# The first half-FFN of a two-layer backbone: latents and context as one operand of 768 tokens, by block products

## The chip, the cores and the metric

The kernel runs on one core of a Trainium2 chip. The metric is the device time of one execution in microseconds (us). TensorE (PE in the profile) multiplies matrices, VectorE (DVE) and ScalarE (ACT) work on SBUF and PSUM, GpSimd (POOL) does little here, and SyncE (SP) issues all loads and stores, in order. Results of TensorE land in 8 PSUM banks of 128 x 512 fp32 values.

## The reference

512 latent tokens `x` and 256 context tokens `ctx`, of width 1024, pass two layers. Each layer is a half-step SwiGLU, a token mixer (layer 0: a bidirectional HGRN2 over context and latents; layer 1: a chunked spatial-gating MLP), and a second half-step SwiGLU. The part that is changed is the first half-FFN of layer 0, for both streams with the same weights:

```
def modulate(x, m, k):                       # m = silu(cond) @ w_mod + b_mod, 9 chapters of 1024
    return x * (1 + m[3*k+1]) + m[3*k]
def swiglu(h, w_in, w_out):
    gate, up = split(h @ w_in, 2)            # w_in 1024 x 5632, w_out 2816 x 1024
    return (silu(gate) * up) @ w_out
x   = layer_norm(alpha * x   + mx[2] * 0.5 * swiglu(modulate(x,   mx, 0), w_in, w_out))
ctx = layer_norm(alpha * ctx + mc[2] * 0.5 * swiglu(modulate(ctx, mc, 0), w_in, w_out))
```

`mx` comes from the conditioning `c`, `mc` from `c_ctx`; both use the same `w_mod`. Behind it the HGRN2 reads the modulated latents and context.

## The kernel before

fp32 products are made of three matmuls each (`mm3`): an operand is split into a rounded part (ScalarE copies it, L135) and the rest (VectorE subtracts, L136), and hi x hi, hi x lo and lo x hi are added in PSUM. `unit` loads one weight tile of 128 x 1024 (512 KB) into a ring of 3 (`raw`) and splits it into a ring of 6 (`w`).

The hidden width is 22 blocks of 128; a block f needs two units (gate 2f, up 2f+1), each of 8 k-slices. `FeedIn` makes the products of a block plainly: 2 x 8 x 3 matmuls of 128 x 512 for the latents (`psf<-xm,w`), then `evac`: silu of the gate bank on ScalarE, times the up bank on VectorE, kept in SBUF as `h`. `FeedContext` does the same with 256 columns (`psf<-xmc,w`). The order before is: latent feed, latent `OutPhase`, context feed, context `OutPhase`, HGRN values (`psv`). So both weights are loaded and split twice. `OutPhase` runs 22 steps (2 halves of the output columns x 11 pairs of blocks); a step loads one unit of `w_out`, splits two blocks (`hs`), and makes 6 matmuls of 128 x 512 per token tile (`y<-w,hs`). At its end each token tile is gated, added, normalised (`evac`, `norm`) and transposed (`pt`) into the next operand.

At the start the operand is made k by k: two modulation rows per k (chapters 1 and 0) are multiplied with silu(c) on VectorE (`mod_dot`, two half dots of 512 and a read of the accumulator), and the columns scale and shift the transposed tokens. The first six units are staged: their products are made k by k in six banks as the slices of `xm` arrive. The other modulation chapters are queued and taken a row at a time (`mod_step`) between blocks.

The later half-FFNs use `FeedSums`: two units that share a block are combined so that seven products of blocks (half of k by 256 columns) replace eight (`seven`). It needs sums of operand blocks (`f4` to `f7`, made once in `sum_steps`) and of weight halves per pair (`weight_sums`, four half-width operations on VectorE), and keeps four partial banks in `sc`. Per pair of units 84 matmuls replace 96. In the second half-FFN of layer 0 (`f2`) the operand's blocks `bw` have eight tiles of their own.

A scheduler orders the instructions of each engine within the program order and the pools; a tile's slot is reused when all its readers are done. The names: `xm`/`xmc` the split operands, `hs` the split products, `mraw`/`mw` modulation rows, `raw`/`rawu` gate and up weights as loaded, `e` a weight sum, `psf` plain banks, `psc`, `pse`, `psa`, `psb` banks of `seven`.

Of the kernel before, what the change touches and what calls it, by code (L numbers as in the profile page):

```python
# [1 line left out]

# [36 lines left out]
SEG = NT + NTC  # L39
NLATE = 4  # L40
# [30 lines left out]
def backbone_kernel(  # L71
# [92 lines left out]
    def mod_dot(pool, dst, w, s):  # L164

        n = D // 2
        for i in range(2):
            c = slice(i * n, (i + 1) * n)
            junk = pool.tile([P, n], BF16, tag="junk", name="junk", bufs=2)
            nc.vector.scalar_tensor_tensor(junk, w[:, c], 1.0, s[:, c], ALU.mult, ALU.mult, dst[:, i : i + 1])  # L170

    def mod_task(modp, srow, l, ch, conds):
        accs = {c: modp.tile([P, KD, 2], F32, tag=f"acc_{c}", name=f"acc_{c}", bufs=2) for c in conds}
        for f in range(KD):
            raw = modp.tile([P, D], F32, tag="mraw", name="mraw", bufs=2)
            nc.sync.dma_start(raw, mod_w[l, ch, f])
            for c in conds:
                mod_dot(modp, accs[c][:, f, :], raw, srow[c])
            yield
        for c in conds:  # L180
            key = (l, ch, c)
            dot = modp.tile([P, KD], F32, tag="dot", name="dot", bufs=2)
            nc.vector.reduce_sum(dot, accs[c], axis=AX.X)
# [14 lines left out]
    class Scraps:  # L198
# [5 lines left out]
        def tile(self, shape, dtype, tag, name, bufs=1):  # L204
            if tag == "mraw":
                return self.pool.tile(shape, dtype, tag=self.ring, name=self.ring, bufs=2)
            got = self.got.setdefault(tag, [0])
            n = int(np.prod(shape[1:])) * (2 if dtype == BF16 else 4) // 4
# [393 lines left out]
    class Forms:  # L602
# [7 lines left out]

        def place_forms(self, new_block):
            self.new_block, self.blocks, self.place = new_block, {}, ExitStack()
# [40 lines left out]
        def blocks_of(self, xm):  # L653
            h = KD // 2
            return (xm[:, :, k0 : k0 + h, c0 : c0 + 2 * P] for k0, c0 in ((0, 0), (h, 0), (h, 2 * P)))
# [9 lines left out]
        def seven(self, xm, sp, raw0, raw1, sc, early=None):  # L665
# [5 lines left out]
            K2, N2 = D // 2, 2 * P  # L671
# [16 lines left out]
            def raws():  # L688
# [4 lines left out]
                return g, u, sp.tile([P, D], F32, tag="e", name="e", bufs=2)  # L693
# [114 lines left out]
    class HgrnValues(Phase):  # L808
# [7 lines left out]
        def load(self):  # L816
            self.ws = [unit(hg_wi[0, kk]) for kk in range(4)]
# [155 lines left out]
    xm = new_xm(xmp, "xm", T)  # L973
    L0 = ExitStack()
    xcp = L0.enter_context(sbuf(name="xcp", bufs=1))
    xmc = new_xm(xcp, "xmc", TC)

    with sbuf(name="hp", bufs=1) as hp, sbuf(name="modp", bufs=1) as modp:
        nc.scalar.preload_act_table(AF.Silu)
        srow = {"x": silu_row(modp, "x")}  # L980

        f0 = FeedIn(0, 0, xm, NT, 6)
        with sbuf(name="first", bufs=1) as fp:
            cols = fp.tile([P, KD, 2], F32, name="cols")
            f0.open()
# [5 lines left out]

            def feed(k):
                acc = fp.tile([P, 2, 2], F32, tag="acc", name="acc", bufs=2)
                xt = fp.tile([P, T], F32, tag="xt", name="xt", bufs=3)
                for ch in (1, 0):
                    m = fp.tile([P, D], F32, tag="mw", name="mw", bufs=6)
                    for c in ((slice(0, D // 2), slice(D // 2, D)) if k == 0 else (slice(0, D),)):
                        nc.sync.dma_start(m[:, c], mod_w[0, ch, k][:, c])
                    mod_dot(modp, acc[:, ch, :], m, srow["x"])
# [8 lines left out]
            bias = fp.tile([P, KD, 2], F32, name="bias")  # L1008
            for ch in range(2):
                nc.vector.tensor_scalar(bias[:, :, ch], mbT[:, 0, ch, :], float(ch), None, ALU.add)  # L1010
            for k in range(KD):
                acc, xt = fed if k == 0 else feed(k)
                nc.vector.reduce_sum(cols[:, k, :], acc, axis=AX.X)
                nc.vector.tensor_tensor(cols[:, k, :], cols[:, k, :], bias[:, k, :], ALU.add)
# [3 lines left out]
                else:  # L1018
# [4 lines left out]
                    xf = fp.tile([P, T], F32, name="xf")  # L1023
                    nc.vector.tensor_scalar(xf, xt, cols[:, k, 1:2], cols[:, k, 0:1], ALU.mult, ALU.add)
                    latest[0] = nc.vector.tensor_tensor(xm[:, 1, k, :], xf, hi.bitcast(F32), ALU.subtract)
# [9 lines left out]
            products(KD - 1, staged)  # L1035
        nc.sync.dma_start(lnT, ln_T)
        srow["c"] = silu_row(modp, "c")
        for ch in (2, 4, 3):
            queue_mod(modp, srow, 0, ch, ["x", "c"])
        for ch in (1, 0):  # L1040
            queue_mod(modp, srow, 0, ch, ["c"])
        for l, ch in ((0, 5), (0, 7), (0, 6), (0, 8), (1, 2)):
            queue_mod(modp, srow, l, ch, ["x"])
        hget = f0.rest(hp, 2)
        with bpools() as bp:

            def context_operand():
                sc, sh = made((0, 1, "c")), made((0, 0, "c"))
                for k in range(KD):
                    ct = bp.tile([P, TC], F32, tag="ct", name="ct", bufs=2)  # L1050
                    nc.sync.dma_start(ct, ctxT[k])
                    nc.vector.tensor_scalar(ct, ct, sc[:, k : k + 1], sh[:, k : k + 1], ALU.mult, ALU.add)
                    split(xmc[:, 0, k, :], xmc[:, 1, k, :], ct)

            f1 = FeedContext(0, 0, xmc, NTC)
            xm = new_xm(xmp, "xm", T)
            OutPhase(
                hget, NF, ffn_units(0, 0), NT, 0, 0, "x", 0.5, lambda t: x[t], False, (0, 1),
                xm, lambda t: x1[t], f1,
            ).run(bp, context_operand, 1)  # L1060
            hget = f1.rest(hp, 0.5)
            for ch in (5, 7, 6):
# [564 lines left out]
```

## Time and profile before

| | |
|---|---|
| three runs | 2439.37, 2439.59, 2440.41 us; median 2439.59 |
| profiled execution | span 2438.5 us (the page gives its span; no other time of it is recorded) |
| TensorE, weight loads | 2410.2 us (99%), 2187.7 us (90%) |
| VectorE, ScalarE, GpSimd | 1959.6 us (80%), 1174.1 us (48%), 35.7 us (1%) |
| chain that ended last | TensorE 91%, VectorE 5% |
| transfers | 366 MB, 150 GB/s over the span |

A line of a group reads: line of the kernel, engine, operation, tile written <- tiles read, shapes, count | busy us, mean ns of one | idle time before them and what ended it. A timeline row reads: start, duration, engine, line, operation, in brackets the idle time before. Row of stretches: for each engine the busy time and the number of instructions, then granted clock, share of the DMA engines and GB/s.

### The profile page before, as it was taken

How to read it: one execution, taken by the hardware profiler on the slowest of the kernel's cores; microseconds unless marked ns; L12 is line 12 of the kernel's file. 1: busy time of each engine (PE TensorE's matmuls, PEld its weight loads, DVE VectorE, ACT ScalarE, POOL GpSimd, SP SyncE). 2: the span in 40 equal slices, each digit the busy share in tenths (PEclk: the TensorE clock that was granted, in tenths of full speed). 3: DMA queues.
4: the chain of work that ended last, by engine and by line, in shares of the span. 5: the costliest groups of instructions: out<-in, count | busy, mean ns of one | idle time of the engine just before them, and what ended most of it. 6: DMA issues, size and time to landing. Idle time of an engine off the chain costs nothing.

```text
span 2438.5 us, 38322 instructions
## 1 busy us (share of the span) xinstructions
PE 2410.2 (99%) x14979; PEld 2187.7 (90%) x14979; DVE 1959.6 (80%) x3522; ACT 1174.1 (48%) x1830; POOL 35.7 (1%) x57
## 2 busy tenths in 40 slices
PE   7999999999999999999999999999999999999998
PEld 5888889988889888999988999988999988999987
DVE  7965678786488886988896988898888887988785
ACT  4222434454355452555643555534666643555641
POOL 0000000000000000000000000000000000000000
PEclk9999999999999999999999999999999999999999
DMA  8866555874212213433474333574322365333452
GB/s 322 293 211 204 167 177 184 290 259 158 70 53 62 65 48 113 160 107 108 145 234 151 104 105 104 163 247 155 116 87 92 124 234 163 132 112 104 139 165 77
DMA packets 107431, 366.04 MB, mean 150 GB/s; under 512 B 12472, under 2 KB 13808, under 8 KB 107248
## 3 DMA queue, kind: packets, MB, share of 16 engines
q1 hardware_dynamic: 107248, 363.58, 45.2%
q8 instruction: 117, 1.92, 0.3%
q14 instruction: 66, 0.54, 0.1%
HBM read 350.92 MB, written 12.61 MB: 149 GB/s over the span
## 4 chain that ended last, share of the span: by engine, by line
PE 91%; DVE 5%; DMA 1%; ACT 1%; issue 1%; POOL 0%; SPq 0%; DVEq 0%; POOLq 0%; ACTq 0%
PE y L150 9%; PE y L148 9%; PE y L149 9%; PE psf L150 5%; PE psf L148 5%; PE psf L149 5%; PE psc L148 5%; PE psc L150 5%; PE psc L149 5%; PE pse L150 3%; PE pse L148 3%; PE pse L149 2%; PE psa L149 1%; PE psa L150 1%; PE psa L148 1%; PE psq L150 1%
## 5 line engine op out<-in xcount | busy, mean ns | idle before, releaser
L135 ACT ACTIVATE w<-raw 128x1024 fp32r<-128x1024 f32 (+3 forms) x447 | 435.1, 976 | 399.0 <-DMA raw<-in_ffn_w_in 85.3
L136 DVE TENSOR_TENSOR w<-raw,w 128x1024 fp32r<-128x1024 f32 (+3 forms) x447 | 499.5, 1121 | 154.6 <-ACT w L135 153.6
L148 PE MATMUL y<-w,hs 128*128 128x512 f32 x984 | 383.7, 390 | 0.0
L150 PE MATMUL y<-w,hs 128*128 128x512 f32 x984 | 383.1, 389 | 0.2 <-DVE hs L136 0.2
L149 PE MATMUL y<-w,hs 128*128 128x512 f32 x984 | 382.9, 389 | 0.0
L135 ACT ACTIVATE hs<-h 128x512 fp32r<-128x512 f32 (+1 forms) x220 | 125.9, 587 | 198.6 <-PE y L150 181.0
L150 PEld LDWEIGHTS y<-w,hs 128*128 128x128 f32 x984 | 184.6, 188 | 39.6 <-DVE hs L136 1.2
L149 PEld LDWEIGHTS y<-w,hs 128*128 128x128 f32 x984 | 184.7, 188 | 38.2
L148 PEld LDWEIGHTS y<-w,hs 128*128 128x128 f32 x984 | 184.7, 188 | 38.2
L148 PE MATMUL psf<-xm,w 128*128 128x512 f32 (+1 forms) x544 | 191.3, 356 | 14.6 <-ACT xm L1021 11.0
L150 PE MATMUL psf<-xm,w 128*128 128x512 f32 (+1 forms) x544 | 192.4, 354 | 1.3 <-DVE w L136 1.2
L149 PE MATMUL psf<-xm,w 128*128 128x512 f32 (+1 forms) x544 | 192.1, 354 | 0.4 <-DVE xm L136 0.4
L136 DVE TENSOR_TENSOR hs<-h,hs 128x512 fp32r<-128x512 f32 (+1 forms) x220 | 134.9, 632 | 68.7 <-ACT hs L135 68.6
L148 PE MATMUL psc<-f,w 128*128 128x256 f32 x560 | 159.0, 284 | 0.9 <-ACT sc L728 0.9
L150 PE MATMUL pse<-f,w 128*128 128x256 f32 x560 | 158.8, 283 | 0.0
L148 PE MATMUL pse<-f,w 128*128 128x256 f32 x560 | 158.5, 283 | 0.0
L150 PE MATMUL psc<-f,w 128*128 128x256 f32 x560 | 158.5, 283 | 0.0
L149 PE MATMUL psc<-f,w 128*128 128x256 f32 x560 | 158.5, 283 | 0.0
L149 PE MATMUL pse<-f,w 128*128 128x256 f32 x560 | 158.4, 283 | 0.0
L148 PE MATMUL psc<-xm,w 128*128 128x256 f32 x548 | 156.3, 285 | 0.6 <-ACT sc L728 0.5
L150 PE MATMUL psc<-xm,w 128*128 128x256 f32 x548 | 155.0, 283 | 0.0
L149 PE MATMUL psc<-xm,w 128*128 128x256 f32 x548 | 155.0, 283 | 0.0
(343 smaller groups left out, 6020.5 us busy)
## 6 DMA issues: line engine op xcount, KB each, us to landing
raw<-in_ffn_w_in SPq DMA_DIRECT2D x159, 512.0 KB, 4.6
raw<-in_ffn_w_out SPq DMA_DIRECT2D x110, 512.0 KB, 4.0
mraw<-in_mod_w SPq DMA_DIRECT2D x80, 512.0 KB, 4.6
rawu<-in_mod_w SPq DMA_DIRECT2D x64, 512.0 KB, 3.6
rawu<-in_ffn_w_in SPq DMA_DIRECT2D x60, 512.0 KB, 3.7
x<-x SPq DMA_DIRECT2D x36, 512.0 KB, 4.4
raw<-in_hg_wf SPq DMA_DIRECT2D x32, 512.0 KB, 3.6
raw<-in_cm_w_out SPq DMA_DIRECT2D x24, 512.0 KB, 4.3
```

The costliest lines, as they stand in the source:

```text
L135: latest_hi[0] = nc.scalar.activation(dst_hi, src, AF.Copy)
L136: latest[0] = nc.vector.tensor_tensor(dst_lo, src, dst_hi.bitcast(F32), ALU.subtract)
L148: nc.tensor.matmul(ps, ah, bh, start=start, stop=False, **kw)
L149: nc.tensor.matmul(ps, ah, bl, start=False, stop=False, **kw)
L150: return nc.tensor.matmul(ps, al, bh, start=False, stop=stop, **kw)
```

## The change

Latents and context become one operand `xa` of 768 columns (`xm` its first 512, `xmc` its last 256). Blocks 0 to 5 stay plain: 48 matmuls of 512 for the latents at the start (0 to 2 staged, 3 to 5 after) and 48 of 256 for the context at the end. Blocks 6 to 21, 16 pairs, are made by `seven` over all 768 tokens, with blocks of 384 columns. All products are stored to DRAM (`hd`) and read back (`hl`, 44 loads of 384 KB) by one output phase `BothOut` over six token tiles, each step loading one unit of `w_out` for both streams. So `w_out` and the input weights of the 16 pairs are loaded and split once for both streams; those of blocks 0 to 5 still twice.

The context's columns are not queued any more: the 16 rows of the start are kept (`mrows`, `mw`), and 16 dots of 1024 (`acc_c`) run on them after the last latent slice. `mod_dot` is one operation of 1024 everywhere. The context's affine and splits and the block sums follow, then the first pair. HGRN's values and states are cut from one tile `held`, and the blocks of `f2` from one tile `blocks` in the slot of `xa`, instead of eight tiles in a pool of their own.

```
-        n = D // 2
-        for i in range(2):
-            c = slice(i * n, (i + 1) * n)
-            junk = pool.tile([P, n], BF16, tag="junk", name="junk", bufs=2)
-            nc.vector.scalar_tensor_tensor(junk, w[:, c], 1.0, s[:, c], ALU.mult, ALU.mult, dst[:, i : i + 1])
+        junk = pool.tile([P, D], BF16, tag="junk", name="junk", bufs=1)[:, : w.shape[1]]
+        nc.vector.scalar_tensor_tensor(junk, w, 1.0, s, ALU.mult, ALU.mult, dst)
...
+    hd = dram.tile([NF, P, TA], F32, name="hd")
+    class FeedBoth(Forms, FeedIn):
+        N2, ne = TS, 1                                  # TS = 384
...
+        def evac(self, hp, f, psg, psu, c0, c1):
+            c = slice(c0, c1)
+            s = hp.tile([P, TA], F32, tag="silu", name="silu", bufs=1)
+            nc.scalar.activation(s[:, c], psg[:, : c1 - c0], AF.Silu)
+            h = hp.tile([P, TA], F32, tag="h", name="h", bufs=3)
+            nc.vector.tensor_tensor(h[:, c], psu[:, : c1 - c0], s[:, c], ALU.mult)
+            nc.sync.dma_start(hd[f][:, c], h[:, c])
...
+        def by_sums(self, hp, sp, f, early=None):
+            sc = sp.tile([P, 4, TS], F32, tag="sc", name="sc", bufs=1)
...
+            pa, pe, pc, pb = self.seven(
+                self.xa, sp, self.src(2 * f), self.src(2 * f + 1), [sc[:, i, :] for i in range(4)], early
+            )
...
+            nc.vector.tensor_tensor(h, h, s, ALU.mult)
+            nc.sync.dma_start(hd[f], h)
+    class BothOut(OutPhase):
+        def operands(self, hf, kk):
+            w, hs = unit(self.units(hf, kk)), []
+            for i in range(2):
+                raw = self.hl.tile([P, TA], F32, tag="hl", name="hl", bufs=3)
+                nc.sync.dma_start(raw, hd[2 * kk + i])
+                s = next(self.ring)                     # 7 slots
+                split(s[:, 0, :], s[:, 1, :], raw)
+                hs.append(s)
+            return w, hs
...
+            self.lead(0, npair - 2, nmod)
+            self.load_gate(0)
+            held = [(kk, *self.operands(0, kk)) for kk in range(npair - 2, npair)]
+            for t in range(nt):
+                for h in held:
+                    self.part(0, *h, [t])
+                self.evac(0, t)
+            self.load_gate(1)
+            self.lead(1, npair - self.tail, nmod)
...
+            nxt.load(3)
+            for t in range(nt):
+                for h in held:
+                    self.part(1, *h, [t])
+            for p in range(2):
+                done(p)
+                for kb in range(KD // 2):
+                    self.operand(p, kb)
+            nxt.load(1)
+            nxt.ahead(0)
+            done(2)
...
+            for k in [*range(KD // 2, KD), *range(KD // 2)]:
+                for ch in (1, 0):
+                    mod_dot(fp, acc_c[:, k, ch : ch + 1], row(k, ch), srow["c"])
+            ccols = const.tile([P, KD, 2], F32, name="ccols")
+            nc.vector.tensor_tensor(ccols, acc_c, bias, ALU.add)
...
+            for f in range(3):
+                f0.evac(hp, f, f0.pss[2 * f], f0.pss[2 * f + 1], 0, T)
+            ctx_steps = context_operand()
+            for f in range(3, NPLAIN):                  # NPLAIN = 6
+                f0.plain(hp, f, xm, 0, T)
...
+            for f in range(NPLAIN, NF):
+                f0.by_sums(hp, sp, f, steps if f == NPLAIN else None)
...
+                mod_step(1)
+            for f in range(NPLAIN):
+                f0.plain(hp, f, xmc, T, TA)
+                mod_step(1)
...
+            BothOut(ffn_units(0, 0), xa, hv).run(bp, hl, 2)
...
-            f2 = FeedSums(0, 1, None, NT, lambda i: bw.tile([P, 2, 2 * P], F32, name=f"bw{i}"))
+            f2 = FeedSums(0, 1, None, NT, lambda i: blocks[i])
...
+            flat = xap.tile([P, 2 * KD * TA], F32, tag="xa", name="blocks")[:, 2 * KD * TA - n :]
+            blocks.extend(flat.rearrange("p (i k t) -> p i k t", k=2, t=2 * P)[:, i] for i in range(KD))
```

VectorE's order right behind the last latent slice, before (`cols` are the last latent columns, `h` the evacuations of the staged banks, `junk,acc_x` queued modulation dots):

```order
L1014 TENSOR_TENSOR cols<-cols,bias 128x2
L136 TENSOR_TENSOR xm<-xt,xm 128x512
L582 TENSOR_TENSOR h<-psf,silu 128x512
L136 TENSOR_TENSOR w<-raw,w 128x1024
L582 TENSOR_TENSOR h<-psf,silu 128x512
L136 TENSOR_TENSOR w<-raw,w 128x1024
L582 TENSOR_TENSOR h<-psf,silu 128x512
L170 SCALAR_TENSOR_TENSOR junk,acc_x<-mraw,srow_x 128x512 x2
```

And now, on the same engine, from the last of the weight splits on (five more splits, eight `acc_c` dots on `mw` and one on `mrows` stand ahead of the first row):

```order
L140 TENSOR_TENSOR w<-raw,w 128x1024
L171 SCALAR_TENSOR_TENSOR junk,acc_c<-mrows,srow_c 128x1024 x7
L1231 TENSOR_TENSOR ccols<-acc_c,bias 128x16
L1237 TENSOR_SCALAR blk<-blk,ccols 128x256 x2
L1041 TENSOR_TENSOR h<-psf,silu 128x512
L1237 TENSOR_SCALAR blk<-blk,ccols 128x256
L140 TENSOR_TENSOR xa<-blk,xa 128x2x256
L1041 TENSOR_TENSOR h<-psf,silu 128x512
```

The first evacuation has moved from right behind the last latent split to behind sixteen dots, six weight splits and two context affines.

SyncE's queue where the second half-FFN of layer 0 begins, before (`x_84<-x` stores the latents, `rawu` is a pair's up-weight; in brackets the semaphores a transfer waits for):

```order
L690 DMA raw<-in_ffn_w_in 128x1024 [waits DMAHW2_49,DVE_49]
L692 DMA rawu<-in_ffn_w_in 128x1024 [waits DMAHW3_49]
L496 DMA x_84<-x 128x1024 [waits DMAHW4_49,DVE_49]
L496 DMA x_84<-x 128x1024 [waits DMAHW5_49,DVE_49]
L692 DMA rawu<-in_ffn_w_in 128x1024 [waits DMAHW6_49]
L690 DMA raw<-in_ffn_w_in 128x1024 [waits DMAHW7_49,DVE_49,Activation_49]
```

And now:

```order
L694 DMA raw<-in_ffn_w_in 128x1024 [waits DMAHW4_49,DVE_49,Activation_49]
L498 DMA x_84<-x 128x1024 [waits DMAHW5_49,DVE_49]
L696 DMA rawu<-in_ffn_w_in 128x1024 [waits DVE_49,DMAHW6_49,PE_49,Activation_49]
L696 DMA rawu<-in_ffn_w_in 128x1024 [waits DMAHW7_49]
L413 DMA x<-x_84 128x1024 [waits DMAHW0_49]
L413 DMA x<-x_84 128x1024 [waits DMAHW1_49]
```

The first up-weight has moved behind all four stores, and has got waits on VectorE, ScalarE and TensorE: it waits for the last reader of `blocks`, VectorE's last split of a block.

More of the change, by code (lines that the diff above doesn't have):

```diff
@@ L39 @@
 SEG = NT + NTC
+TA = T + TC
+TS = TA // 2
+NPLAIN = 6
 NLATE = 4
@@ L181, in mod_task @@
             key = (l, ch, c)
[L182 to L183 removed]
+            dot = accs[c]
             if ch % 3 == 2:
@@ L206, in tile @@
                 return self.pool.tile(shape, dtype, tag=self.ring, name=self.ring, bufs=2)
+            n = int(np.prod(shape[1:])) * (2 if dtype == BF16 else 4) // 4
+            if tag != "junk" and self.small.shape[1] < D:
+                return self.pool.tile(shape, dtype, tag=tag, name=name, bufs=bufs)
             got = self.got.setdefault(tag, [0])
-            n = int(np.prod(shape[1:])) * (2 if dtype == BF16 else 4) // 4
             if got[0] < bufs and tag != "junk" or len(got) == 1:
@@ L814, in __init__, with load @@
             self.xm, self.ps = xm, {}
-        def load(self):
-            self.ws = [unit(hg_wi[0, kk]) for kk in range(4)]
+        ws = ()
+        def load(self, n):
+            self.ws = [*self.ws, *(unit(hg_wi[0, kk]) for kk in range(len(self.ws), len(self.ws) + n))]
         def tok(self, src, t):
@@ L979, in backbone_kernel @@
+    xa, xm, xmc = new_xa()
+    with ExitStack() as e_sc:
         nc.scalar.preload_act_table(AF.Silu)
-        srow = {"x": silu_row(modp, "x")}
-        f0 = FeedIn(0, 0, xm, NT, 6)
+        f0 = FeedBoth(0, 0, xa, xm, xmc)
+        early = ExitStack()
+        f0.blk = early.enter_context(swap("blk")).tile([P, KD, TA], F32, name="blk")
         with sbuf(name="first", bufs=1) as fp:
+            srow = {"x": silu_row(fp, "x")}
             cols = fp.tile([P, KD, 2], F32, name="cols")
+            acc_c = fp.tile([P, KD, 2], F32, name="acc_c")
+            bias = fp.tile([P, KD, 2], F32, name="bias")
+            xf = fp.tile([P, T], F32, name="xf")
+            rows = xmp.tile([P, KD, D], F32, tag="xm", name="mrows")
@@ L1035, in backbone_kernel @@
             products(KD - 1, staged)
-        nc.sync.dma_start(lnT, ln_T)
[L1037 to L1062, printed above, removed]
-                made((0, ch, "x"))
-            xmc = new_xm(xcp, "xmc", TC)
-            hv = HgrnValues(xm)
-            OutPhase(
-                hget, NF, ffn_units(0, 0), NTC, 0, 0, "c", 0.5, lambda t: ctx_tok[t], False, (0, 1),
-                xmc, None, hv,
-            ).run(bp, None, 0.5)
-            for l, ch in ((0, 8), (1, 2)):
@@ L1071, in backbone_kernel @@
+        with bpools() as bp, sbuf(name="hl", bufs=1) as hl:
+            xa, xm, xmc = new_xa()
+            hv = HgrnValues(xm)
+            BothOut(ffn_units(0, 0), xa, hv).run(bp, hl, 2)
+            for l, ch in ((0, 5), (0, 7), (0, 6), (0, 8), (1, 2)):
                 made((l, ch, "x"))
@@ L1117, in backbone_kernel @@
             nc.scalar.activation(lnoml, oml, AF.Ln)
-            v = [hg.tile([P, D], F32, name=f"v{s}") for s in range(SEG)]
             for cb in range(2):
```

183 lines of the change are left out of this document (160 added, 23 removed).

## The prediction

> **What bounds the kernel now.** I read the page's totals first, then the chain that ended last, then stretches of the first 560 us and of the second half-FFN (which already multiplies by block products), then who TensorE waits for.
>
> ```profile
> span 2438.5 us, 38322 instructions
> PE 2410.2 (99%) x14979; PEld 2187.7 (90%) x14979; DVE 1959.6 (80%) x3522; ACT 1174.1 (48%) x1830; POOL 35.7 (1%) x57
> PE 91%; DVE 5%; DMA 1%; ACT 1%; issue 1%; POOL 0%; SPq 0%; DVEq 0%; POOLq 0%; ACTq 0%
> ...
> core 0: us, PE busy (x) PEld busy (x) DVE busy (x) ACT busy (x) POOL busy (x), PEclk, DMA share, GB/s
> 0.00:11.00 11.00, 0.00 (x0) 0.00 (x0) 3.83 (x16) 3.48 (x5) 0.69 (x6) 1.00 0.85 280
> 11.00:108.00 97.00, 93.11 (x391) 74.52 (x392) 86.63 (x219) 38.74 (x49) 0.00 (x0) 1.00 0.89 319
> 400.00:509.00 109.00, 109.00 (x911) 109.00 (x910) 80.57 (x130) 48.50 (x63) 0.00 (x0) 1.00 0.86 282
> 1010.00:1300.00 290.00, 289.08 (x2049) 272.96 (x2049) 251.49 (x399) 158.62 (x261) 0.00 (x0) 1.00 0.48 157
> ...
> PE psf L148 <- ACT xm L1021: 11.0, 1, 11.0
> PE psf L148 <- ACT w L135: 3.0, 1, 3.0
> PE psf L150 <- DVE w L136: 0.8, 1, 0.8
> ```
>
> TensorE is the bound: 99% busy, 91% of the chain. Of its 28.3 us without work, 14.8 lie before 24 us (the last three rows); the rest of the first half-FFN has next to none. So time goes with TensorE's own work, and every new gap on TensorE is paid in full. Two rows give bounds for what comes: the context's feed (400 to 509) kept TensorE at 109.00 of 109.00 while 282 GB/s were moved, and the second half-FFN's block products (1010 to 1300) kept it at 289.08 of 290 with VectorE at 87%.
>
> The profiled execution spans 2438.5 us; the median of the runs is 2439.59, 1.1 us more. I make the sum against the span and add 1.1.
>
> **Change, first part: fewer columns through TensorE.** Matmuls are pipelined, so the price of one is the distance between starts in an unbroken run.
>
> ```profile
> 284.83 0.39 PE L150 MATMUL y<-w,hs 128*128 128x512 f32 x1
> ...
> 311.81 0.39 PE L149 MATMUL y<-w,hs 128*128 128x512 f32 x1
> ...
> 439.75 0.28 PE L148 MATMUL psf<-xmc,w 128*128 128x256 f32 x1
> ...
> 451.99 0.28 PE L148 MATMUL psf<-xmc,w 128*128 128x256 f32 x1
> ...
> 1715.24 0.33 PE L148 MATMUL pscv<-w,xm 128*128 128x384 f32 x1
> ...
> 1718.88 0.33 PE L148 MATMUL pvc<-w,xm 128*128 128x384 f32 x1
> ```
>
> 512 columns: 119 steps from the first to the second row, 26.98 us, 0.2267. 256: 102 steps in 12.24, 0.120. 384: 21 steps in 3.64, 0.1733. Before, the feed is 22 blocks of 48 matmuls of 512 for the latents and 48 of 256 for the context: 1056 x 0.2267 + 1056 x 0.120 = 239.4 + 126.7 = 366.1 us. After: six plain blocks of each kind, 288 x 0.2267 + 288 x 0.120 = 65.3 + 34.6, and 16 pairs of 84 matmuls (seven products of four k, three each) of 384 columns, 1344 x 0.1733 = 233.0; together 332.9. That is **33.2 us less**, and the most the change can bring. The 792 output matmuls, the 48 transposes and the value products stay.
>
> **Hidden in the steady stages.** A pair lasts 84 x 0.1733 = 14.6 us. VectorE does in it 3.5 weight splits of 1024 (1.13 between starts, below: 4.0), four half-width weight sums (2.4), three evacuations of 384 and one of 768 (2.5) and two modulation dots of 1024 (2.3): 11.2 of 14.6, 77%, where 87% cost 0.9 us in 290. Its transfers, two weights, one modulation row and the store of the products, are 1.9 MB, 130 GB/s. In the output phase one of 22 steps is 36 matmuls, 8.15 us; it loads one weight (512 KB), two products back from DRAM (768 KB) and mostly two modulation rows (1 MB): 2.36 MB, 289 GB/s, hardly more than the 282 that 400 to 509 carried without a TensorE gap. I take zero for both, and up to 5 us at the phase's entry, where six token loads stand in SyncE's queue ahead of the third step's products: I take 0.5, since TensorE has two steps (16 us) in hand.
>
> **Second part: a new stretch on VectorE after the start.** The context's columns are now 16 dots of 1024 on the kept modulation rows, right behind the last latent column and ahead of the first evacuation of the staged banks. Their rows:
>
> ```profile
> L136 DVE TENSOR_TENSOR w<-raw,w 128x1024 fp32r<-128x1024 f32 x131 | 159.2, 1221 | 51.7 <-ACT w L135 51.6
> L170 DVE SCALAR_TENSOR_TENSOR junk<-mraw,srow_x 128x512 bf16<-128x512 f32 x122 | 79.2, 684 | 2.9 <-DMA mraw<-in_mod_w 2.9
> L1052 DVE TENSOR_SCALAR ct<-ct,mc_c,mc_c 128x256 f32<-128x256 f32 x8 | 3.1, 412 | 6.5 <-DMA ct<-in_ctxT 6.5
> L136 DVE TENSOR_TENSOR w<-raw,w 128x768 fp32r<-128x768 f32 x20 | 18.6, 948 | 3.6 <-ACT w L135 3.5
> ...
> 43.22 0.69 DVE L170 SCALAR_TENSOR_TENSOR junk<-mw,srow_x 128x512 bf16<-128x512 f32 x1
> ...
> 43.83 0.69 DVE L170 SCALAR_TENSOR_TENSOR junk<-mw,srow_x 128x512 bf16<-128x512 f32 x1
> ...
> 47.27 0.69 DVE L136 TENSOR_TENSOR xm<-xt,xm 128x512 fp32r<-128x512 f32 x1 [2.35 <-ACT xm L135]
> 49.91 0.69 DVE L582 TENSOR_TENSOR h<-psf,silu 128x512 f32<-128x512 f32 x1 [1.94 <-ACT silu L580]
> ...
> 52.60 1.22 DVE L136 TENSOR_TENSOR w<-raw,w 128x1024 fp32r<-128x1024 f32 x1
> 53.73 0.68 DVE L582 TENSOR_TENSOR h<-psf,silu 128x512 f32<-128x512 f32 x1
> ...
> 52.02 0.39 PE L150 MATMUL psf<-xm,w 128*128 128x512 f32 x1
> ...
> 11.00:52.00 41.00, 37.12 (x143) 28.25 (x144) 33.51 (x87) 19.26 (x25) 0.00 (x0) 1.00 0.91 351
> ```
>
> A half dot takes 0.61 between starts, so a whole one lies between 1.13 (a 1024-wide operation) and 1.22 (two halves); I take 1.14, near the one instruction it now is. The last latent split ends at 47.9. Behind it VectorE has 15 dots (17.1), six weight splits of blocks 3 to 5 (6.8), the columns (0.2) and two context affines (0.7), then the first evacuation (0.6): done at 73.3, where before it began at 49.91. TensorE ends the staged products at 52.2 (143 matmuls to 52.0, and one), has banks for three more units, and reaches the fourth, which needs the evacuated bank, at 52.2 + 72 x 0.2267 = 68.5. It waits **4.8 us**. Should the earlier columns come sooner (one dot instead of two, no reduce: up to 2 us), 2.8; with 1.22 per dot and a late weight, 8.
>
> From there VectorE still has 5 evacuations (3.0), 6 affines (2.2), 4 context splits (2.4), 8 block sums and 6 splits of 768 (0.87 each by the 948 ns row: 12.2), and of the early pair's weights two splits of 1024, two of 512 and three sums (5.3): 25.1, and by estimate 1.6 of waits for ScalarE's halves, so its third weight is split at 100.0. TensorE gets there at 73.3 + 16.3 (three units) + 48 x 0.1733 = 97.9, and waits **2.1 us** (0 to 4). Both together 6.9, with ends 2.8 and 12.
>
> **Third part: the two joins behind.** With one output phase, the value products come straight behind 32 transposes (3.5 us) with nothing else to put between.
>
> ```profile
> L403 DVE TENSOR_SCALAR pt<-pt,opc 128x256 f32<-128x256 f32 x8 | 4.0, 537 | 0.0
> ...
> 995.29 1.22 DVE L136 TENSOR_TENSOR w<-raw,w 128x1024 fp32r<-128x1024 f32 x1
> 996.43 2.49 DVE L630 TENSOR_TENSOR bw<-bw,bw 128x512 f32<-128x512 f32 x4
> ...
> 977.08 0.42 SPq L692 DMA_DIRECT2D rawu<-in_ffn_w_in  x1
> ...
> 1008.97 0.28 PE L148 MATMUL pse<-f,w 128*128 128x256 f32 x1
> ...
> rawu<-in_ffn_w_in SPq DMA_DIRECT2D x60, 512.0 KB, 3.7
> ```
>
> Behind the last output matmul VectorE has the last token's first step (0.6), five affines (0.46 each, 537 ns overlapped) and the first split (0.6): about 3.8 us against 3.5 of transposes, behind which ScalarE's splits alternate: **1.0** (0.3 to 3).
>
> At the second half-FFN the blocks lie in one tile that also frees the space of the up-weights, so the first such load now waits for the last block split. VectorE from 995.29: a split (1.13), eight sums and eight splits of 512 (0.61 each, 9.8), with none of the weight sums between that stand there now: done at 1006.2. Load 3.7, weight sum 0.6, ScalarE's half split 0.6: 1011.1, where TensorE needs it at 1008.97; before it was issued at 977.08 at the latest. 2.1, and about 0.9 more until the full up-weight is split: **3.0** (1 to 7). Beyond this point TensorE's list is the same; VectorE's dots are joined, which nothing waits for.
>
> **Sum.** -33.2 + 6.9 + 0.5 + 1.0 + 3.0 = -21.8; 2438.5 - 21.8 + 1.1 = 2417.8, say 2418. Shorter start, 8 MB fewer modulation rows: nothing, since TensorE's backlog runs to 52.2 anyway.
>
> **A rule on the clock.** After the start's gap TensorE ran slowly though the granted clock reads 1.00:
>
> ```profile
> 16.00 0.80 PE L148 MATMUL psf<-xm,w 128*128 128x512 f32 x1 [3.01 <-ACT w L135]
> ...
> 20.84 0.47 PE L149 MATMUL psf<-xm,w 128*128 128x512 f32 x1
> ...
> 21.38 0.40 PE L148 MATMUL psf<-xm,w 128*128 128x512 f32 x1
> 21.61 0.39 PE L149 MATMUL psf<-xm,w 128*128 128x512 f32 x1
> ```
>
> Twelve matmuls from 16.00 to 20.84 took 4.84 us instead of 2.7: 2.1 us lost. If each of my three gaps of 2 us and over did that, 6.3 us come on top: 2424. The Trainium skill ("TensorE: Matmul & The Clock Gate", Part 1 and "HAM oscillation") says that an idle window of about 3.4 us halves the clock until about 3.4 us of work; by that rule the 4.8 us gap may pay once, and the others not. The rows fit it, though 3.01 with three matmuls ahead is a start and no gap in full work.
>
> **Rivals.** (a) As summed, 2412 to 2424: 0.50. (b) Waits mostly covered: the dots run faster, the columns come early, the load is short; 3 us of waits in all leave 2438.5 + 1.1 - 33.2 + 3 = 2409, range 2406 to 2412: 0.17. For it: the start's VectorE has slack (2.35 and 1.94 us in the rows). Against: 16 dots are 18 us in one queue. (c) Larger waits: clock halved at three gaps, 8 us at the evacuation, 3 at the entry, 5 at the second half-FFN: 2424 to 2434: 0.20. (d) Slower: the way over DRAM. Each of 22 steps needs its two products from SyncE's queue, behind weights and modulation rows, at the 289 GB/s above. With 11.4 us of waits granted as summed, 21.8 us are left; from 1.0 us a step (9.15 instead of 8.15, that is, 258 GB/s) it is even, and from 1.2 (252 GB/s) slower than before by 0.2%; at 1.8 it ends at 2457. Against: 400 to 509 held 282 with full TensorE. For: that stretch wrote nothing back and read nothing that it had written. 0.08. (e) Even, between (c) and (d): 0.05.
>
> A difference under 0.2% (4.9 us) can't be told from none here. Faster: (a), (b), (c): 0.87; same 0.05; slower 0.08. The range takes (b) nearly whole and (c): 2407 to 2434, leaving out (d), (e) and some of (b).
>
> **What would show it.** Right: matmuls of 384 columns 0.173 apart; no TensorE wait inside the pairs; one wait of 3 to 6 us on the evacuated bank near 68 us, one near 98 us on the up-weight's split, one near 985 us (shifted) on the block product's weight, with the up-weight's load issued just ahead of it. Wrong: waits for the products read back, repeated in every step of the output phase; pairs longer than 14.6 us; 384-column steps over 0.18; slow matmuls behind each gap.

## The result, and the profile after

The median is 2453.1 us (2449.71 to 2454.11) against 2440.0 of the kernel before in the same runs: ratio 1.0053, 95% interval 1.0038 to 1.0067. The changed kernel is slower by 13 us; forecast were 22 less. The page of the profile after, its first lines and its GB/s in 40 slices of 61 us (the output phase lies in the seventh to ninth):

```profile
span 2450.2 us, 37518 instructions
PE 2383.5 (97%) x14787; PEld 2188.1 (89%) x14787; DVE 1985.2 (81%) x3173; ACT 1180.3 (48%) x1835; POOL 37.5 (2%) x57
...
GB/s 308 153 144 143 129 249 312 311 208 123 84 52 61 61 52 103 151 121 104 139 236 147 113 107 104 150 258 141 129 85 89 127 214 174 131 118 104 139 163 77
```

TensorE is busy 26.7 us less (2383.5, was 2410.2), but the span is 11.7 longer: its time without work grew from 28.3 to 66.7 us. The 26.7 us are less than the 33.2 that the columns save: matmuls whose starts lie about twice as far apart as usual (half pace below; last section) count as busy, and the three spells of them behind new waits take some 5.4 us. The waits of TensorE, longest first:

```profile
PE pg L187 <- DVE acc_x L185: 19.8, 1, 19.8
PE psf L152 <- ACT xa L1211: 10.9, 1, 10.9
PE psf L152 <- ACT w L139: 5.8, 2, 4.2
PE pse L152 <- ACT sc L732: 3.3, 1, 3.3
PE psf L152 <- DVE h L1041: 3.1, 1, 3.1
PE pse L152 <- ACT w L139: 2.3, 1, 2.3
PE psf L152 <- ACT silu L1039: 1.9, 1, 1.9
```

The first line is new and is half of the growth: the transposition of a finished modulation chapter (`pg`), which waits for VectorE's sum of that chapter. VectorE, SyncE and TensorE around it:

```profile
585.93 1.22 DVE L171 SCALAR_TENSOR_TENSOR junk<-mraw,srow_x 128x1024 bf16<-128x1024 f32 x1 [2.84 <-DMA mraw<-in_mod_w]
...
595.62 1.23 DVE L171 SCALAR_TENSOR_TENSOR junk<-mraw,srow_x 128x1024 bf16<-128x1024 f32 x1 [1.15 <-DMA mraw<-in_mod_w]
596.77 0.08 DVE L171 DVE_READ_ACCUMULATOR junk<-mraw,srow_x 128x1 f32 x1
596.89 0.17 DVE L185 TENSOR_TENSOR acc_x<-acc_x,mbT 128x8 f32<-128x8 f32 x1
...
580.37 2.79 SPq L177 DMA_DIRECT2D mraw<-in_mod_w  x2
...
587.19 5.08 SPq L177 DMA_DIRECT2D mraw<-in_mod_w  x3
...
577.11 0.27 PE L187 MATMUL pg<-ident,acc_x 128*8 128x128 f32 x1
597.20 0.37 PE L187 MATMUL pg<-ident,acc_x 128*8 128x128 f32 x1 [19.82 <-DVE acc_x L185]
```

The last queued chapter still has rows to load and multiply when the output phase is over, in the middle of the value products, with TensorE's transposition ahead of the rest of these products in its queue. It is the first gate of layer 1 (the last entry, `(1, 2)`, of the loop behind `BothOut` in the kernel that calls `made` for each queued chapter). Nothing near it reads this gate: the kernel asks for it there because the buffers of the queue end there. The modulation rows by stretch (pairs; context blocks; output phase; behind it), each row one dot and one read of the accumulator, or two of each where it serves both streams:

```profile
92.00:333.00 241.00, 44.18 (x72) 1.00 0.44 146
333.00:367.40 34.40, 14.76 (x24) 1.00 0.92 312
367.40:548.60 181.20, 39.35 (x64) 1.00 0.80 278
548.60:597.00 48.40, 9.83 (x16) 0.84 0.47 152
```

The first 24 rows serve both streams, so these are 18, 6, 32 and 8 rows (as the program is written 16, 6, 34 and 8; two are made ahead of their stage). The 16 instructions of the last line are 8 rows for one stream: a whole chapter came too late.

In the other stages that I had counted as hidden, TensorE has work nearly all the time, though VectorE is busy for 53.77 of 61 us in the pairs, 88%, where I had added up 77%. Pairs, and two stretches of the output phase (us, PE, PEld, DVE, ACT, POOL, granted clock, DMA share, GB/s):

```profile
122.00:183.00 61.00, 61.00 (x353) 60.78 (x352) 53.77 (x76) 28.93 (x44) 0.00 (x0) 1.00 0.44 145
...
367.00:429.00 62.00, 60.88 (x271) 50.04 (x271) 38.41 (x57) 17.14 (x19) 0.00 (x0) 1.00 0.89 311
429.00:490.00 61.00, 61.00 (x271) 50.52 (x270) 51.12 (x70) 22.84 (x26) 0.00 (x0) 1.00 0.90 311
```

### The profile page after: what moved, and what is told of

Same layout as the page of the kernel before. It is cut to its first block, busy times and chain, and to the rows that moved or that the text cites. A ratio compares the mean times of both kernels' runs of the same rounds, so it can differ in the third digit from the quotient of the medians.

```text
span 2450.2 us, 37518 instructions
## 1 busy us (share of the span) xinstructions
PE 2383.5 (97%) x14787; PEld 2188.1 (89%) x14787; DVE 1985.2 (81%) x3173; ACT 1180.3 (48%) x1835; POOL 37.5 (2%) x57
## 4 chain that ended last, share of the span: by engine, by line
PE 54%; DVE 3%; DMA 1%; ACT 0%; issue 0%; POOL 0%; SPq 0%; DVEq 0%; POOLq 0%
PE y L154 6%; PE y L153 6%; PE y L152 6%; PE psc L152 5%; PE psc L154 5%; PE psc L153 5%; PE pse L154 3%; PE pse L152 3%; PE pse L153 3%; PE psa L154 1%; PE psa L153 1%; PE psa L152 1%; PE pscs L1710 1%; PE pvc L154 1%; PE pvc L152 1%; PE pvc L153 1%
## 5 line engine op out<-in xcount | busy, mean ns | idle before, releaser
L139 ACT ACTIVATE w<-raw 128x1024 fp32r<-128x1024 f32 (+3 forms) x393 | 371.7, 949 | 359.3 <-DMA raw<-in_ffn_w_out 102.8
L140 DVE TENSOR_TENSOR w<-raw,w 128x1024 fp32r<-128x1024 f32 (+3 forms) x393 | 425.9, 1088 | 138.5 <-ACT w L139 137.7
L152 PE MATMUL pse<-f,w 128*128 128x256 f32 (+1 forms) x688 | 202.0, 294 | 5.6 <-ACT sc L732 3.3
L152 PE MATMUL psc<-f,w 128*128 128x256 f32 (+1 forms) x688 | 201.8, 293 | 1.7 <-ACT sc L732 1.7
L154 PE MATMUL pse<-f,w 128*128 128x256 f32 (+1 forms) x688 | 202.3, 294 | 0.2 <-DVE w L140 0.2
L153 PE MATMUL pse<-f,w 128*128 128x256 f32 (+1 forms) x688 | 201.6, 293 | 0.0
L153 PE MATMUL psc<-f,w 128*128 128x256 f32 (+1 forms) x688 | 201.3, 293 | 0.0
L154 PE MATMUL psc<-f,w 128*128 128x256 f32 (+1 forms) x688 | 201.2, 292 | 0.0
L732 ACT ACTIVATE sc<-psc 128x256 f32<-128x256 f32 (+1 forms) x238 | 96.3, 404 | 150.8 <-PE psc L154 137.0
L140 DVE TENSOR_TENSOR w<-rawu,w 128x1024 fp32r<-128x1024 f32 x86 | 105.2, 1223 | 54.2 <-ACT w L139 53.6
L152 PEld LDWEIGHTS pse<-f,w 128*128 128x128 f32 x688 | 132.0, 192 | 6.4 <-ACT sc L732 4.0
L139 ACT ACTIVATE hs<-h 128x512 fp32r<-128x512 f32 x132 | 80.3, 628 | 113.9 <-PE y L154 98.7
L152 PEld LDWEIGHTS psc<-f,w 128*128 128x128 f32 x688 | 131.6, 191 | 2.5 <-ACT sc L732 2.5
```

What stands on the lines that cost most here:

```text
L139: latest_hi[0] = nc.scalar.activation(dst_hi, src, AF.Copy)
L140: latest[0] = nc.vector.tensor_tensor(dst_lo, src, dst_hi.bitcast(F32), ALU.subtract)
L152: nc.tensor.matmul(ps, ah, bh, start=start, stop=False, **kw)
L153: nc.tensor.matmul(ps, ah, bl, start=False, stop=False, **kw)
L154: return nc.tensor.matmul(ps, al, bh, start=False, stop=stop, **kw)
L732: self.copies.append(nc.scalar.activation(sc[i], ps[:, :N2], AF.Copy, scale=scale))
```

## The experiments

Every span below is that of one profiled execution; the kernel before has 2438.5, the changed kernel 2450.2. "First value matmul" is the first one behind the value products (`psfl`): 636.9 before, 643.2 after.

**Rows earlier.** The pairs take one and a half rows each instead of one, so that 8 more are done before the output phase.

```
             for f in range(NPLAIN, NF):
                 f0.by_sums(hp, sp, f, steps if f == NPLAIN else None)
-                mod_step(1)
+                mod_step(1.5)
```

> Edit: the pairs take 1.5 queued modulation rows each instead of 1 (24 rows instead of 16), so that 64 of 64 rows are taken before the output phase ends, instead of 56. Theory L (late chapter): the 19.8 us wait of the transposition pg among the value products is the last chapter's eight rows, loaded and multiplied only behind the output phase; it goes, and with it the half-speed matmuls behind it (about 16 of 0.43 instead of 0.227, 3.4 us). Span about 2450 - 23 = 2427, under the kernel before. Rival C (crowding): the end of the one output phase leaves VectorE and SyncE so far behind that the value products wait anyway, on the operand or the weights; then pg no longer waits, but 10 us or more of waits stand elsewhere between 545 and 640, and the span stays above 2437. A second rival: eight more rows make the pairs' VectorE the bound (12.3 of 14.6 us): pairs longer than 14.6 us, some 5 us lost.

Median 2431.58 us, ratio 0.9966 (0.9954 to 0.9979): faster than the kernel before. The span is 2429.0, 21.2 less than after; `psfl` begins at 622.3, 20.9 earlier. `pg` no longer waits, and the stretch that had held the gap is full:

```profile
577.00:612.00 35.00, 35.00 (x156) 28.88 (x155) 10.28 (x23) 8.47 (x13) 1.06 (x4) 1.00 0.35 122
```

So the late chapter is shown to be the cause of the loss, with 19.8 us of wait and about 2.3 in the eleven slow matmuls behind it. Neither rival holds: the only wait of 1 us or more between 545 and 640 us is one of 1.8 at the first value product, and TensorE is busy for 61.00 of 61 us in the pairs (122 to 183), with VectorE at 59.63. Asking for this gate later, without more rows in the pairs, was not run.

**No pairs at all.** On top of that, all 22 blocks plain for both streams; the way over DRAM and the one output phase stay.

```
-            for f in range(3, NPLAIN):
+            for f in range(3, NF):
                 f0.plain(hp, f, xm, 0, T)
...
-            for f in range(NPLAIN, NF):
-                f0.by_sums(hp, sp, f, steps if f == NPLAIN else None)
...
-            for f in range(NPLAIN):
+            for f in range(NF):
                 f0.plain(hp, f, xmc, T, TA)
```

> Edit on top of the rows taken early: no pair goes by sums, all 22 blocks are plain for latents and context; the spill to DRAM and the one output phase stay (rows: one per latent block from the seventh on, 0.7 per context block). TensorE's work grows by 16 x 48 x (0.2267 + 0.120) - 1344 x 0.1733 = 266.3 - 233.0 = 33.3 us. The waits of the first pair (5 us) go. Theory P (the price of the products is as forecast): 28 us above e1, about 2455. Rival: if the sums' stage loses time that no wait shows (384 columns slower than 0.1733), the difference is clearly smaller than 28; if merging itself costs much, this kernel ends far over the kernel before: over 2460.

2454.66 us, span 2452.9: 23.9 more than with pairs, `psfl` 25.8 later. TensorE's saving is there: it is busy for 2415.0 us, against 2383.5 with pairs; the span gains less than the 33.2 of the columns because the pairs bring the waits of the first pair with them.

This kernel ends 14.4 us behind the kernel before, but that is not the price of the joint output phase, since it also carries the context's dots. Up to `psfl` (648.1, 11.2 later than before) its rows show 1.8 us more of waits at the start, 4.6 at the evacuated bank with 2.6 of half pace behind them, and 1.75 at the value products: 10.7 of the 11.2. So the joint phase with its way over DRAM neither gains nor costs much by itself.

**Context ahead.** Three of the six context blocks are made before the first pair, so that VectorE has 17 us more for the block sums and the first weights.

```
+            for f in range(3):
+                f0.plain(hp, f, xmc, T, TA)
             for f in range(NPLAIN, NF):
...
-            for f in range(NPLAIN):
+            for f in range(3, NPLAIN):
                 f0.plain(hp, f, xmc, T, TA)
-                mod_step(1)
+                mod_step(2)
```

> Edit on top of the rows taken early: three of the six plain context blocks are made ahead of the first pair instead of behind the last one. Theory B (backlog): the two waits in the first pair (3.3 and 1.8 us) are VectorE's queue of context columns, splits and block sums, which ends near 103 us; 17.3 us more of TensorE's work ahead of the pair cover it, and both waits go: about 5 us less than e1, 2422. The waits ahead of it (1.9 on the gate bank, 3.1 on the up bank) stay. Rival S (ScalarE's order): the copies of the first pair stand behind a weight split and the silu rows in ScalarE's queue whatever the time; then the waits stay within 1 us.

Span 2422.9 (run 2424.6), 6.1 less than with the rows alone; the wait of 3.3 on `sc` at the first pair is gone. What had held it, ScalarE in the kernel with the rows earlier (first three rows) and VectorE in it:

```profile
98.95 0.47 ACT L732 ACTIVATE sc<-psc 128x384 f32<-128x384 f32 x1
104.01 1.58 ACT L139 ACTIVATE w<-raw 128x512 fp32r<-128x512 f32 x2 [4.59 <-DVE raw L723]
105.49 0.47 ACT L732 ACTIVATE sc<-pse 128x384 f32<-128x384 f32 x1
...
101.56 1.82 DVE L140 TENSOR_TENSOR f<-blk,f 128x768 fp32r<-128x768 f32 x2
103.29 0.68 DVE L723 SCALAR_TENSOR_TENSOR raw<-raw,e 128x512 f32<-128x512 f32 x1
```

The copy of the second product stands in ScalarE's queue behind the split of the fourth weight, and that waits 4.59 us for VectorE, which is still at the block sums.

**Is it ScalarE's order?** Two tries on the kernel with the rows earlier. In the first the fourth weight's sum and split are written behind the copies:

```
             product(pc, we, K2, self.f6, False, True)
             kept(2, pc)
             if early:
+                nc.vector.scalar_tensor_tensor(g[:, lo], g[:, hi], -1.0, e[:, hi], ALU.mult, ALU.subtract)
+                w4 = weights(g, K2)
```

> Compared with the version whose pairs take 1.5 modulation steps each (span 2429.0). Only the place of the early pair's fourth weight changes: its sum and its split are written behind the second and third copies of that pair's products, so ScalarE meets the copies first. Theory Q (the wait of 3.3 us at 106 us is ScalarE's in-order queue: the copy stands behind the fourth weight's half split): the wait falls to 0.5 us or less, and with it the run of matmuls at half rate behind it (the 384-column steps at 0.32 instead of 0.17, about 2.7 us); first value matmul 4 to 6 us earlier, span 2423 to 2425. Rival W (the weight itself is late, VectorE's backlog): about 3 us of wait stay at that place or one product later, under the name of a weight, and the span stays within 1 us of 2429.

Span 2429.4, the same wait of 3.27. The scheduler put the instructions back where they had been, so this says nothing on the order; it is a second profile of the same kernel. In the next the split is tied behind the third copy (`with tc.issue_after(self.copies[2].ins): w4 = weights(g, K2)`):

> Compared with the version whose pairs take 1.5 modulation steps (span 2429.0; 2429.4 where the written place of the fourth weight was changed and no engine's order was). Now ScalarE's half split of the early pair's fourth weight is tied behind the third copy of that pair's products, so that its queue really is another. Theory Q (ScalarE's order): the copy of the second product runs as soon as TensorE has it, near 102.7, the wait of 3.3 us at 106 us is gone or under 0.5, and its half-rate steps (0.32 instead of 0.17) with it; first value matmul 3 to 6 us earlier, span 2423 to 2426. Rival W (a backlog: the fourth weight is now late itself): 2 us or more of wait on a weight at the pair's last product, about 112 us, and the span within 1.5 us of 2429. Between the two if the copy behind it, which stands behind the row's silu at 108.6, keeps its wait.

The wait stayed, 3.6 us, and the span was 2435.9. ScalarE again stood still with another instruction of VectorE's at its head:

```profile
98.93 0.47 ACT L730 ACTIVATE sc<-psc 128x384 f32<-128x384 f32 x1
104.45 0.52 ACT L1064 ACTIVATE silu<-silu 128x384 f32<-128x384 f32 x1 [5.06 <-DVE silu L1063]
104.88 0.47 ACT L730 ACTIVATE sc<-pse 128x384 f32<-128x384 f32 x1
```

So VectorE's backlog up to 104 us reaches TensorE through whatever ScalarE has at the head of its queue, and with less backlog (context ahead) the wait goes. Both forecasts missed: the wait did not fall, and it did not move to the fourth weight at the pair's end. Whether ScalarE's order alone could remove it is not shown, since in both orders an instruction that needs VectorE stands ahead of the copy. This run is 6.9 us longer than the one with the rows alone; 4.7 us of wait at the output phase's entry and about 2.5 of half pace behind it cover that, in a stage that the edit does not touch.

**That entry.** In the versions whose token loads stand where the changed kernel has them, the entry of the output phase waited 1.1 (after), 0 (rows earlier), 0.3, 0 (all plain), 1.7, 4.7 and 5.3 us (this last one in the run told of next). The 0 and the 1.7 belong to kernels with the same order on every engine, so at least that much changes from run to run; each of the others was profiled once. The longest, on SyncE's queue of that kernel and TensorE:

```profile
376.60 1.75 SPq L1124 DMA_DIRECT2D x<-in_x  x4
378.39 2.52 SPq L1124 DMA_DIRECT2D x<-in_ctx_tok  x2
380.96 0.65 SPq L1096 DMA_DIRECT2D hl<-hd  x1
...
392.76 0.79 PE L152 MATMUL y<-w,hs 128*128 128x512 f32 x1 [5.30 <-ACT hs L139]
```

The products' loads (`hl`) stand behind the six token loads. Moving these behind the first four steps (`self.lead(0, 4, nmod)` ahead of the six loads), on the kernel with the context ahead:

> Compared with the version that makes three context blocks ahead of the first pair (span 2422.9, run 2424.6). Only SyncE's order changes: the six loads of the token rows stand behind the loads of the output phase's first four steps instead of ahead of them. Theory S (the wait at the phase's entry, 0.3 to 5.3 us from run to run, is the products' load behind those six loads): that entry shows no wait over 0.5 us, the median of the runs is 0 to 3 us less, 2421 to 2424.5, and the runs lie closer together. Rival (the entry is held by the round trip over DRAM itself, from the store of the last pair's products): the entry's wait stays between 0 and 5 us and the median within 1 us of 2424.6. If the token rows come late instead, VectorE's first step on a token waits, and TensorE's transposes or output banks with it: over 2425.

Median 2423.68 us (2422.05 to 2425.11), ratio 0.9929 (0.9915 to 0.9944); span 2422.1. The entry shows no wait in this kernel nor in the three that were built on it. The gain against the single run of 2424.6 is within its spread; what went, as far as four profiles show, is the risk of up to 5 us.

**Blocks apart.** On the kernel with the rows earlier, `xa` is two tiles and the blocks of the second half-FFN take the slot of the second, so that the first up-weight's load does not wait for the last block split.

```
-        xa = xap.tile([P, 2, KD, TA], F32R, tag="xa", name="xa")
+        xa = Halves([xap.tile([P, KD, TA], F32R, tag=f"xa{i}", name=f"xa{i}") for i in range(2)])
...
-            flat = xap.tile([P, 2 * KD * TA], F32, tag="xa", name="blocks")[:, 2 * KD * TA - n :]
+            flat = xap.tile([P, KD * TA], F32, tag="xa1", name="blocks")[:, KD * TA - n :]
```

> Edit on top of the rows taken early: the joint operand is two tiles (rounded part and rest) instead of one, and the second half-FFN's blocks take the slot of the second only, so that the up-weights' space is free when the first has no reader. Theory W: the wait in the second half-FFN's first pair (2.3 + 0.2 us, and the 3.6 us by which that half-FFN has fallen back against the kernel before) is the first up-weight's load behind the last block split; it goes, 2 to 4 us less than e1. Rival: the weight comes early and VectorE's order (sums ahead of the weights) keeps the pair waiting all the same: no change within 1 us.

Median 2432.79 us, ratio 0.9972 (0.9961 to 0.9983), no better. The load goes out at 980.49 instead of 992.16, and TensorE still waits 1.83 us instead of 2.27. The block splits end at 996.9, but in VectorE's queue the up-weight's sum (`e`, last row) also stands behind two evacuations, which wait for ScalarE, and behind the pair's own first sum, which waits for a product of TensorE:

```profile
980.49 1.14 SPq L696 DMA_DIRECT2D rawu<-in_ffn_w_in  x2
...
994.37 2.49 DVE L140 TENSOR_TENSOR f<-blocks,f 128x512 fp32r<-128x512 f32 x4
997.06 0.69 DVE L584 TENSOR_TENSOR h<-psf,silu 128x512 f32<-128x512 f32 x1 [0.20 <-ACT silu L582]
998.47 0.69 DVE L584 TENSOR_TENSOR h<-psf,silu 128x512 f32<-128x512 f32 x1 [0.72 <-ACT silu L582]
999.94 0.42 DVE L778 TENSOR_TENSOR silu<-psa,sc 128x256 f32<-128x256 f32 x1 [0.78 <-PE psa L154]
1000.28 0.68 DVE L713 TENSOR_TENSOR e<-raw,rawu 128x512 f32<-128x512 f32 x1
```

In the changed kernel the order is the same, and there the late load adds only 0.36 us:

```profile
1016.72 0.69 DVE L713 TENSOR_TENSOR e<-raw,rawu 128x512 f32<-128x512 f32 x1 [0.36 <-DMA rawu<-in_ffn_w_in]
```

A kernel with that sum first was not run, so whether another order alone would remove the wait stays open. The median here also contains the entry's wait of 0 to 5 us, so a gain of some tenths would not show in it.

**Columns split.** On the kernel with the token loads moved, 8 of the 16 dots for the context's columns go behind the three first evacuations (`sc_row` is the silu of the context's conditioning, made a second time).

```
-            for k in [*range(KD // 2, KD), *range(KD // 2)]:
+            for k in range(KD // 2, KD):
                 for ch in (1, 0):
                     mod_dot(fp, acc_c[:, k, ch : ch + 1], row(k, ch), srow["c"])
...
             for f in range(3):
                 f0.evac(hp, f, f0.pss[2 * f], f0.pss[2 * f + 1], 0, T)
+            for k in range(KD // 2):
+                for ch in (1, 0):
+                    nc.vector.scalar_tensor_tensor(
+                        junk_c, row(k, ch), 1.0, sc_row, ALU.mult, ALU.mult, acc_c[:, k, ch : ch + 1]
+                    )
```

> Compared with the version with the token loads moved. Eight of the sixteen dots that make the context's columns are written behind the three first evacuations instead of ahead of them. Theory V (the wait on the evacuated bank near 68 us is VectorE's row of 16 dots of 1.14 us): eight dots less ahead of it are 9 us of VectorE, so the wait of 3.8 and the one of 0.8 behind it fall to 1 us or less together, and the 10 matmuls at half rate behind it (0.43 instead of 0.23, 2.0 us) go as well: 5 to 6 us less, span 2415 to 2418. Rival P (VectorE's whole backlog, not its order, sets it: the eight dots are then paid one place later, at the context blocks or the first pair): a new wait of 2 to 5 us between 75 and 120 us, and 0 to 2 us less in all.

Median **2417.85 us** (2416.19 to 2418.7), ratio 0.9904 (0.9887 to 0.992): the best, and faster than both kernels. Span 2416.7, 5.4 less; between the start and the pairs TensorE waits nowhere over 0.5 us. VectorE's first evacuation (`h`) is where the changed kernel still had 8 dots:

```profile
61.89 1.23 DVE L140 TENSOR_TENSOR w<-raw,w 128x1024 fp32r<-128x1024 f32 x1
63.70 1.23 DVE L140 TENSOR_TENSOR w<-raw,w 128x1024 fp32r<-128x1024 f32 x1 [0.58 <-ACT w L139]
64.84 0.68 DVE L1041 TENSOR_TENSOR h<-psf,silu 128x512 f32<-128x512 f32 x1
```

In the changed kernel that evacuation came at 75.04.

**Half dots at the start.** The latent columns again from two half dots and a sum each (the first slice, k = 0, has them in every version), first on the kernel with the token loads moved, then on the best one.

```
-                    for i, c in enumerate((slice(0, D // 2), slice(D // 2, D)) if k == 0 else (slice(0, D),)):
+                    halves = (slice(0, D // 2), slice(D // 2, D))
+                    for c in halves if k == 0 else (slice(0, D),):
                         nc.sync.dma_start(m[:, c], mod_w[0, ch, k][:, c])
+                    for i, c in enumerate(halves):
```

> Compared with the version with the token loads moved. In the start's feed the columns are made again from two half dots and a sum for each, as in the kernel before, instead of one dot. Theory H (the start's waits grew from 14.9 to 17 us because the single dots end the columns in lumps, so that an affine on ScalarE stands ahead of the second unit's weight split): the waits of the first 26 us fall to 15 to 15.8 us and the span by 1 to 2 us. Rival (the loads' arrival sets the start, the form of the dots does not matter): the waits of the first 26 us stay at 16.5 to 17.3 and the span within 0.7 us; the backlog of TensorE makes it up or the evacuated bank's wait grows by what the start gains, then no change either.

> The version with eight dots behind the evacuations (2417.85 us, span 2416.7) with the start's half dots besides, which by themselves took 2.5 us from the start's waits (15.1 us instead of 17.7) and nothing from the end, the evacuated bank's wait having taken 0.4 more and the rest being lost in half-rate steps. Theory B1 (with the eight dots moved TensorE has no wait between the start and the value products, so that what the start gains stays): first value matmul 2 to 3 us earlier, 2415 to 2416.5. Rival (half dots cost VectorE 8 x 0.1 us and the sums, and the evacuated bank or the first pair waits again): within 1 us of 2417.85 or over it, with a new wait of 1 us or more between 60 and 120 us.

Span 2423.8 (2422.1 without), and 2418.59 us (2417.06 to 2419.68), ratio 0.9908 (0.9892 to 0.9925), against 2417.85. The waits of the first 26 us fall from 17.7 to 16.1 (15.1, as the second expectation has it, was too low) and from 17.8 to 14.8, and `psfl` begins at 615.4 instead of 615.6, and at 610.9 instead of 610.6. So the longer start comes from the joined dots, wholly in the last kernel (14.85 before) and in part in the other, but giving it back brings nothing: it is lost again, by the rows mostly in more matmuls at half pace at the start (about a dozen in the last kernel, about five without; 2.4 us) and in small waits of 0.5 to 1.0.

## Why the prediction was wrong

The step that failed is **the output phase under "Hidden in the steady stages"**, "one of 22 steps ... mostly two modulation rows". It put the rows' price at nothing: I costed their bandwidth and never counted whether the steps take them all. 64 rows are due by the phase's end: 16 go with the pairs, 6 with the context blocks, 42 are left. Two in each of 22 steps would be 44; but only the 17 steps of `lead` take any, the 5 `held` ones (whose products are kept to the end of each half) none, so 34 are taken and 8 are left. They cost 21.2 us, by the run with the rows earlier. No rival named it: I looked for waits on the products read back and on VectorE's queue, not for a queue that the phase had to empty.

Going back through the experiments, the distance from forecast to measurement (2450.2 against a forecast span of 2416.7, 33.5 us) closes: 21.2 for the late chapter, 6.1 at the first pair, 0.8 at the entry, 5.4 for the columns' dots; the kernel with the columns split stands at 2416.7. These are differences of single profiles; by the medians of the runs the steps are 21.5, 7.9 (first pair and entry together) and 5.8 us. That this is the forecast span is partly chance, since that kernel has other waits than those I summed, and four edits more. The terms:

- **TensorE, -33.2: right.** Without the pairs TensorE is busy 31.5 us longer. 384 columns run as forecast: 84 matmuls, one pair, lie between these rows, 14.76 us where 84 x 0.1733 are 14.56; the 19 behind it take 3.29, 0.173 each.

```profile
121.67 0.33 PE L154 MATMUL psa<-xa,w 128*128 128x384 f32 x1
...
136.43 0.33 PE L154 MATMUL psa<-xa,w 128*128 128x384 f32 x1
...
139.72 0.33 PE L152 MATMUL pse<-f,w 128*128 128x384 f32 x1
```

- **Start, nothing: 2.3 us more of waits** (17.15 in the first 26 us, 14.85 before). I had argued that TensorE's backlog covers the start.
- **Evacuated bank, 4.8: the size was right, 1.9 + 3.1 = 5.0,** in part by chance. The 3.1 at 75.78, ahead of the fourth unit, are the wait named. VectorE's first evacuation ended at 75.7, not 73.3: its first dot for the context waited 1.84 us for `srow_c`, and the last dots stood 1.27 apart, not 1.14. TensorE was about 2 us late itself. The 1.9 at 66.96 I had not named: the third unit needs a gate bank, and ScalarE's silu that empties it stands behind a weight copy that waited 1.44 us for its load. The sum left out what follows the gap, about 1.6 us of half pace.
- **First pair, 2.1: measured 3.29 + 1.75 = 5.0.** VectorE's split of the weight that I named began at 100.07 and ended at 101.3 (forecast: done at 100.0). What held TensorE was the second product's copy on ScalarE, a queue that I had not followed.
- **Entry of the output phase, 0.5 (up to 5): 1.1 in this run,** 0 to 5.3 over the runs; the queue named was the right one.
- **Value products, 1.0: 1.3,** and 1.75 in the other kernels.
- **Second half-FFN, 3.0: 2.3, and about 1.3 of half pace: the size near, the mechanism mostly wrong.** The up-weight's load does wait for the last block split (issued at 1013.01), but the up-weight's sum waits only 0.36 us for it, and with the blocks apart, where it does not wait, TensorE still stands 1.83 us. The rest is VectorE's order, which I had not followed past the block splits.
- **Joined dots, "which nothing waits for": not quite.** 1.6 us at 2001 us and 0.7 earlier are new waits. The split that the first waits for stands behind a dot of 1.22 us, where a half dot of 0.69 stood before; that accounts for 0.5 of the 1.6, and the rest is not explained.
- **Rival (d), the way over DRAM, was wrong:** TensorE ran 61.00 of 61 us at 311 GB/s, above the 282 of before. The result has its sign for another reason.
- **The rule on the clock.** From 16.00 to 20.84 there are ten starts, not twelve, so about 2.6 us were lost there, not 2.1. Slow matmuls behind gaps, which I had listed as a sign of being wrong, came behind the 3.1 and the 2.3 us but not behind the 3.3.

## What to carry to other kernels

When work is spread over the steps of a loop in portions, count portions against steps, and see which steps take none; a remainder stands behind the loop, where nothing covers it. Ask also whether the remainder is needed at that place. A wait on a queue in order is followed through every engine whose head can stand still, not only through the one that makes the operand. A gap in TensorE is to be priced with the slow matmuls behind it.

## What the runs showed of the hardware

TensorE runs at half pace after gaps much shorter than I had allowed. Behind the 19.8 us gap, and behind 3.1 us at 75.78 (stretches of the changed kernel, granted clock in the third column from the end; then single matmuls of 512 columns):

```profile
597.00:600.00 3.00, 2.80 (x7) 2.24 (x8) 0.33 (x2) 0.00 (x0) 0.00 (x0) 0.50 0.07 8
600.00:605.00 5.00, 5.00 (x19) 3.99 (x18) 1.65 (x10) 0.24 (x1) 0.00 (x0) 0.78 0.01 1
605.00:612.00 7.00, 7.00 (x33) 5.79 (x32) 3.67 (x3) 4.49 (x6) 0.00 (x0) 1.00 0.21 72
...
76.60 0.63 PE L152 MATMUL psf<-xa,w 128*128 128x512 f32 x1
77.02 0.63 PE L153 MATMUL psf<-xa,w 128*128 128x512 f32 x1
77.45 0.63 PE L154 MATMUL psf<-xa,w 128*128 128x512 f32 x1
```

The starts lie 0.43 apart instead of 0.2267 (0.32 instead of 0.173 at 384 columns, 0.21 instead of 0.12 at 256). Over the eleven traces of after and the experiments, behind the start: 15 of 16 gaps of 2.7 us and over were followed by such a spell, 9 of 12 gaps of 2.0 to 2.3 us, and 1 of 27 gaps of 1.0 to 2.0. A spell lost about 1.3 to 2.7 us, and sometimes began only after 3 to 10 matmuls at full pace. So a gap of 3 us that is followed by one costs 4 to 6, by these sums.

The Trainium skill ("TensorE: Matmul & The Clock Gate", Part 1) puts the halved clock after an idle window of about 3.4 us and says that the window is free-running, and that cold matmuls of 512 columns start 426.7 ns apart. The pace agrees with the 0.43 here, and the scatter and the late beginnings fit a window that runs by itself; but gaps of 2.0 to 2.3 us, well under the figure, were followed by half pace three times in four.
